# Fewer block products in the output projection of a hybrid encoder layer

## The chip, the cores and the metric

The kernel runs on one core of a Trainium2 chip. Its engines each have an instruction queue of their own, worked off in order: TensorE (PE; its weight loads are listed as PEld), VectorE (DVE), ScalarE (ACT), GpSimd (POOL) and SyncE (SP, which here only starts transfers). The metric is the device time of one execution in microseconds. The kernel before took 1609.84 us, the median of three executions (1609.48 to 1610.66).

## The reference

For 256 tokens of width 4096 the layer computes

```
xn    = RMSNorm(x) * norm_g
h     = xn @ w_in                    # 4096 x 14336: c_val, c_glu, c_gate, q, k, v, a_gate
conv  = silu(LayerNorm(dwconv31(c_val * sigmoid(c_glu)))) * silu(c_gate)
attn  = dilated window attention of 16 heads of 128 (three patterns) * silu(a_gate)
y     = x + concat(conv, attn) @ w_out            # 4096 x 4096
```

all in float32. The change concerns the last line, the product of the 256 x 4096 mixed matrix with `w_out`.

## The kernel before

**Products.** Every product is made of matmuls that hold a 128x128 piece of the activations and stream 128x512 of weights. To keep float32 accuracy each operand is split into a high part, rounded to the fast format fp32r (a cast on ACT), and a low part, the rest (a subtraction on DVE). One block product is three matmuls: high by high, low by high, high by low.

**Groups, steps, pairs.** Weights come in groups of 1024 columns: 14 groups of `w_in` (index 0 to 13), then 4 of `w_out` (14 to 17). A group runs over 32 steps of 128 rows of the weight, each step has 2 token halves (s) x 2 column halves (e) x 3 = 12 matmuls. Weights are loaded by SP as pairs of steps (1 MB, `raw`, 3 buffers) and split three steps ahead (`AHEAD`) into `wh` and `wl` (L197, L198). Four accumulators of 128x512 are in use, another four banks of the accumulator memory ("side") serve the attention.

**The mixed matrix.** Its 32 column blocks (k = 0 to 31, 128 columns each, held as 128 x 256 tokens) are the activations of the output groups. Blocks 0 to 15 are the 16 heads, 16 to 31 the conv path. They are split by `mix_split_gen` (L526, L527) into `mh` and `ml`, in the order 0 to 31, and the output groups use them in that order. A conv block is ready once its gate has come out of the last two input groups (12 and 13, kind "gate"), been turned by 16 small ACT copies per 512 columns (L308) and multiplied in on DVE (L410).

**What sets the order.** The program writes each engine's queue by hand. The loop over steps emits matmuls and splits, and at the end of each step calls `pump`, which lets three lanes of side work (attention and gates, mixed splits, conv) emit instructions up to a quota of estimated time for DVE and ACT. Nothing is reordered at run time: an instruction that waits holds up all behind it on its engine.

Of the kernel before, what the change touches and what calls it, by code (L numbers as in the profile page):

```python
# [11 lines left out]
F32 = mybir.dt.float32  # L12
F32R = mybir.dt.float32r
# [4 lines left out]
P = 128  # L18
S = 256
D = 4096  # L20
KT = D // P
# [23 lines left out]
GROUPS += [("gate", gp, C_GATE + 1024 * gp, C_GATE + 1024 * gp + 512) for gp in range(2)]  # L45
N_IN = len(GROUPS)
GROUPS += [("out", og, 1024 * og, 1024 * og + 512) for og in range(4)]

VECS = {"conv_b": 0, "ln_g": 16, "ln_b": 32, "q_g": 48, "k_g": 49}

# [54 lines left out]
def layer_kernel(  # L105
# [5 lines left out]
    vecs,  # L111
    conv_w,
    bias_rows,
    out,
):
    nc = tc.nc
    xs = x[0].rearrange("(s p) d -> p s d", p=P)
# [5 lines left out]
    def t4(name):  # L123
        return sb.tile([P, 4, 256], F32, tag="c4", bufs=15, name=name)
# [48 lines left out]
    def load_pair(j, cuts=(0, 2048), between=None):  # L173

        g, jj = divmod(j, n_pairs)
        if g >= NG:
            return
        if groups[g][0] == "out":
            jj = (jj + n_pairs // 2) % n_pairs
        rt = sb.tile([P, 2048], F32, tag="raw", bufs=RAW, name=f"raw{j}")  # L180
        raw_tiles[j] = rt.rearrange("p (k c) -> p k c", k=2)
        for lo, hi in zip(cuts, cuts[1:]):
            nc.sync.dma_start(rt[:, lo:hi], w[g, jj, :, lo:hi])
            if between and hi == 1024:
                between()

    w_split = {}

    def split_w(n):
        if n >= NG * KT:  # L190
            return
        j, kk = divmod(n, 2)
        src = raw_tiles[j][:, kk]
        wh = sb.tile([P, 1024], F32R, tag="wh", bufs=AHEAD + 1, name=f"wh{n}")
        wl = sb.tile([P, 1024], F32R, tag="wl", bufs=AHEAD + 1, name=f"wl{n}")
        if n:
            nc.scalar.copy(wh, src)  # L197
            nc.vector.tensor_sub(wl, src, wh.bitcast(F32))  # L198
        else:
            a, b = slice(0, 512), slice(512, 1024)  # L200
            nc.vector.tensor_copy(wh[:, a], src[:, a])
            split_x(0)
            nc.scalar.copy(wh[:, b], src[:, b])
            for c in (a, b):
                nc.vector.tensor_sub(wl[:, c], src[:, c], wh[:, c].bitcast(F32))
        w_split[n] = (wh, wl)
        if kk == 1:
            del raw_tiles[j]
            load_pair(j + RAW)
# [307 lines left out]
    mh, ml = {}, {}  # L517
    progress = {"in": -1}

    def mix_split_gen():  # L520
        for kk in range(KT):
            while not (kk in mix_ready and progress["in"] >= kk + 2):
                yield
            h, l = new_split(kk, "m")
            src = mix_ready[kk]
            nc.scalar.copy(h, src)  # L526
            nc.vector.tensor_sub(l, src, h.bitcast(F32))  # L527
            mh[kk], ml[kk] = h, l
            yield 335

    fg, mix_lane, conv_lane = Lane(3), Lane(1), Lane(1)
    fg.add(setup_gen())
# [18 lines left out]
    def add_out(g, e, s, acc, queues=(nc.sync,)):  # L551

        c, n = groups[g][2 + e], 512 // len(queues)
        for i, queue in enumerate(queues):
            t = xr_tiles[(g, e)][:, s, n * i : n * i + n]
            nc.vector.tensor_add(t, t, acc[:, n * i : n * i + n])  # L556
            queue.dma_start(out[0][P * s : P * s + P, c + n * i : c + n * i + n], t)

    def evacuate(g, e, accs):
        kind, idx = groups[g][:2]  # L560
        rstd = state.get("rstd")
        if kind == "out":
            for s in range(2):
                add_out(g, e, s, accs[s])
            return
        if kind == "conv" and e == 1:
            pair = state["sig"]
        else:
            tile_ = t4(f"{kind}{idx}_{e}")
            pair = tile_.rearrange("p a b -> p (a b)").rearrange("p (s c) -> p s c", s=2)  # L570
        for s in range(2):
            t = pair[:, s, :]
            if kind == "conv" and e == 0:
                nc.scalar.activation(t, accs[s], AF.Sigmoid, scale=rstd[s])
                state["sig"], state["sig_tile"] = pair, tile_
            elif kind == "conv":
                nc.vector.scalar_tensor_tensor(t, accs[s], rstd[s], t, op0=ALU.mult, op1=ALU.mult)
            elif kind == "gate" or (kind == "agv" and e == 0):
                nc.scalar.activation(t, accs[s], AF.Silu, scale=rstd[s])
# [22 lines left out]
    def last_products(n):  # L602

        g, k = divmod(n, KT)
        wh, wl = (t[:, 512:] for t in w_split[n])
        for s in range(2):
            a = accs[(g, 1)][s]
            hs, ls = (t[:, P * s : P * s + P] for t in (mh[k], ml[k]))
            nc.tensor.matmul(a, hs, wh, start=False, stop=False)
            nc.tensor.matmul(a, ls, wh, start=False, stop=False)  # L610
            nc.tensor.matmul(a, hs, wl, start=False, stop=True)
            add_out(g, 1, s, a, (nc.scalar, nc.sync) if s else (nc.sync,))

    def products(n, e, part):

        g, k = divmod(n, KT)
        if k == 0 and part == 0:
            accs[(g, e)] = [
                ps.tile([P, 512], F32, tag="acc", bufs=4, name=f"acc{g}_{e}_{s}") for s in range(2)
            ]  # L620
        if g < n_in:
            h, l = xh[k], xl[k]
        else:
            while k not in mh:
                pump()
            h, l = mh[k], ml[k]
        wp = w_split[n][part][:, 512 * e : 512 * e + 512]
        for s in range(2):
            a = accs[(g, e)][s]
            hs, ls = h[:, P * s : P * s + P], l[:, P * s : P * s + P]  # L630
            if part == 0:
                nc.tensor.matmul(a, hs, wp, start=k == 0, stop=False)  # L632
                nc.tensor.matmul(a, ls, wp, start=False, stop=False)  # L633
            else:
                nc.tensor.matmul(a, hs, wp, start=False, stop=k == KT - 1)  # L635
        if part == 1:
            if k == KT - 1:
                evacuate(g, e, accs.pop((g, e)))
            if e == 1:
                del w_split[n]  # L640

    nc.scalar.dma_start(first_x, x_cols[:, 0 : KT + S])
    xT[0] = first_x[:, KT:]
# [11 lines left out]
    split_w(0)  # L655
    split_x(1)
    split_w(1)
    for n in range(NG * KT):
        g, k = divmod(n, KT)
        if g == n_in - 1:  # L660
            progress["in"] = k
        elif g >= n_in:
            progress["in"] = KT + 2
        if groups[g][0] == "out" and k in (8, 12):
            e = (k - 8) // 4
            c = groups[g][2 + e]
            t = t4(f"xr{g}_{e}").rearrange("p a b -> p (a b)").rearrange("p (s c) -> p s c", s=2)
            nc.sync.dma_start(t, xs[:, :, c : c + 512])
            xr_tiles[(g, e)] = t
        if n == 0:  # L670
            for part in range(2):
                for e in range(2):
                    products(n, e, part)
            for m in (2, 3):
                split_x(m)
                split_w(m)
            rstd_steps = finish_rstd()
        else:
            products(n, 0, 0)
            if k == KT - 1:  # L680
                products(n, 0, 1)
# [5 lines left out]
            split_w(n + AHEAD)  # L687
            if k < KT - 1:
                products(n, 0, 1)
            elif n < NG * KT - 1:  # L690
                products(n, 1, 0)
                products(n, 1, 1)
            else:
                last_products(n)
        if n % 4 == 0 and 12 + n < KT:
            load_xT(12 + n, 4, nc.sync)
        if n in XN_LOAD:
# [7 lines left out]
        elif n == 29:  # L705
            list(rstd_steps)
        pump()

def _layout(i):
# [55 lines left out]
```

## Time and profile before

| | |
|---|---|
| median of three executions | 1609.84 us |
| the profiled execution, its own time | 1610.65 us |
| its span, first to last instruction | 1608.9 us |
| PE busy | 1602.5 us of the span |
| DVE busy | 1072.5 us |
| ACT busy | 926.4 us |
| input groups end, output groups begin on PE | 1256.6 us from the start |
| last matmul starts | 1604.57 us |

Busy times are from the profiled execution. "Idle before" in a row of the groups is the time the engine sat still just before instructions of that group, followed by what released it. A duration is an instruction's own; where an engine overlaps the end of one with the start of the next, the distance between starts is shorter than the duration. Matmuls overlap most: each lasts some 0.39 us, yet they start about 0.23 us apart.

### The profile page before, as it was taken

Reading aid. Unit: us, or ns where it says so; the run is one execution under the profiler, and the core shown is the slowest. Engines: PE = TensorE matmul, PEld = TensorE weight load, DVE = VectorE, ACT = ScalarE, POOL = GpSimd, SP = SyncE. Lnnn points to the kernel's source line nnn. Section 1 sums busy time; section 2 is a strip of 40 time slices with the busy share of each in tenths; the row PEclk is TensorE's granted clock in tenths of the full one; section 3 lists DMA queues with packets and bytes.
Section 4 is the critical chain, followed back from the end, with each engine's and each line's share of the span. In section 5 each row is a group of like instructions: output and inputs, shape, how many; then the busy total and the mean of one; then the engine's idle time right before and its main releaser. Section 6 shows DMA issues by size and latency. Waiting matters only on the chain.

```text
span 1608.9 us, 18840 instructions
## 1 busy us (share of the span) xinstructions
PE 1602.5 (100%) x7058; PEld 1326.6 (82%) x7058; DVE 1072.5 (67%) x1442; ACT 926.4 (58%) x1413; POOL 0.2 (0%) x4
## 2 busy tenths in 40 slices
PE   9999999999999999999999999999999999999999
PEld 7888888888888888888888888888888888888887
DVE  6658888888888888678756555555465665454543
ACT  6763544545453456774778756774767963333332
POOL 0000000000000000000000000000000000000000
PEclk9999999999999999999999999999999999999999
DMA  9755555555555555545555555455555556566662
GB/s 372 291 185 201 191 189 203 185 185 206 187 205 184 196 197 193 193 168 199 185 195 187 187 198 197 174 189 202 184 198 188 196 204 231 207 228 216 216 229 105
DMA packets 52892, 323.53 MB, mean 201 GB/s; under 512 B 5792, under 2 KB 8480, under 8 KB 16192
## 3 DMA queue, kind: packets, MB, share of 16 engines
q1 hardware_dynamic: 52512, 322.05, 56.0%
q8 instruction: 55, 0.90, 0.2%
q10 hardware_dynamic: 288, 0.28, 0.1%
q14 instruction: 37, 0.30, 0.1%
HBM read 318.08 MB, written 4.23 MB: 200 GB/s over the span
## 4 chain that ended last, share of the span: by engine, by line
PE 98%; ACT 1%; DMA 0%; issue 0%; DVE 0%; DVEq 0%
PE acc L632 32%; PE acc L633 32%; PE acc L635 32%; PE psc L469 1%; PE po L508 1%; ACT cT L394 0%; ACT wh L197 0%; DMA first_x<-in_x_cols_dram 0%; ACT qk L308 0%; DVE wl L198 0%; DVE xr L556 0%; DVE qk L449 0%; ACT xh L245 0%; PE vapm L366 0%; PE mupm L366 0%
## 5 line engine op out<-in xcount | busy, mean ns | idle before, releaser
L198 DVE TENSOR_TENSOR wl<-raw,wh 128x1024 fp32r<-128x1024 f32 x575 | 703.6, 1224 | 514.3 <-ACT wh L197 510.4
L197 ACT CAST wh<-raw 128x1024 fp32r<-128x1024 f32 x575 | 604.9, 1053 | 638.4 <-PE acc L633 449.4
L632 PE MATMUL acc<-wh,xh 128*128 128x512 f32 x1792 | 703.9, 393 | 1.0 <-ACT xh L245 1.0
L633 PE MATMUL acc<-wh,xl 128*128 128x512 f32 x1792 | 698.6, 390 | 0.0
L635 PE MATMUL acc<-wl,xh 128*128 128x512 f32 x1792 | 484.1, 389 | 0.0
L632 PEld LDWEIGHTS acc<-wh,xh 128*128 128x128 f32 x1792 | 336.9, 188 | 71.0 <-ACT xh L245 1.3
L633 PEld LDWEIGHTS acc<-wh,xl 128*128 128x128 f32 x1792 | 337.0, 188 | 70.4 <-DVE xl L246 0.2
L635 PEld LDWEIGHTS acc<-wl,xh 128*128 128x128 f32 x1792 | 336.8, 188 | 70.5
L340 DVE SCALAR_TENSOR_TENSOR cT<-conv,wT,cT 128x241 f32<-128x241 f32 (+14 forms) x480 | 201.6, 471 | 0.0
L632 PE MATMUL acc<-wh,mh 128*128 128x512 f32 x510 | 198.4, 389 | 0.0
L633 PE MATMUL acc<-wh,ml 128*128 128x512 f32 x510 | 198.4, 389 | 0.0
L635 PE MATMUL acc<-wl,mh 128*128 128x512 f32 x510 | 137.5, 389 | 0.0
L633 PEld LDWEIGHTS acc<-wh,ml 128*128 128x128 f32 x510 | 95.8, 188 | 19.9
L635 PEld LDWEIGHTS acc<-wl,mh 128*128 128x128 f32 x510 | 95.7, 188 | 19.8
L632 PEld LDWEIGHTS acc<-wh,mh 128*128 128x128 f32 x510 | 95.7, 188 | 19.8
L499 ACT COPY pr<-turn_p 32x128 f32<-32x128 f32 x256 | 75.9, 296 | 5.9 <-DVE turn_p L493 2.4
L308 ACT COPY qk<-turn_q 32x256 f32<-32x256 f32 x64 | 25.9, 404 | 1.2
L308 ACT COPY qk<-turn_k 32x256 f32<-32x256 f32 x64 | 25.8, 403 | 1.2 <-DVE turn_k L300 0.2
L308 ACT COPY gate<-turn_g 32x256 f32<-32x256 f32 x64 | 25.9, 404 | 1.0
L308 ACT COPY agv<-turn_ag 32x256 f32<-32x256 f32 x64 | 25.8, 404 | 1.0
L308 ACT COPY conv<-turn_a 32x256 f32<-32x256 f32 x64 | 25.8, 403 | 1.1
L483 ACT ACTIVATE pr<-pr,nm 128x256 f32<-128x256 f32 x32 | 16.0, 502 | 2.5 <-DVE nm L480 2.4
(128 smaller groups left out, 402.2 us busy)
## 6 DMA issues: line engine op xcount, KB each, us to landing
raw<-in_w_dram SPq DMA_DIRECT2D x286, 1024.0 KB, 4.8
x<-in_x_dram SPq DMA_DIRECT2D x8, 512.0 KB, 7.4
xr<-in_x_dram SPq DMA_DIRECT2D x8, 512.0 KB, 5.8
out_dram<-xr SPq DMA_DIRECT2D x15, 256.0 KB, 5.2
xT<-in_x_cols_dram SPq DMA_DIRECT2D x7, 512.0 KB, 7.3
T<-bias_dram SPq DMA_DIRECT2D x16, 192.0 KB, 5.0
raw<-in_w_dram SPq DMA_DIRECT2D x3, 512.0 KB, 6.5
raw<-in_w_dram SPq DMA_DIRECT2D x2, 256.0 KB, 4.2
```

The lines of the kernel that those rows point to most:

```text
L197: nc.scalar.copy(wh, src)
L198: nc.vector.tensor_sub(wl, src, wh.bitcast(F32))
L308: nc.scalar.copy(dst[32 * b : 32 * b + 32, :, :, to, :], backwards(v) if flip else v)
L340: nc.vector.scalar_tensor_tensor(c[:, t, lo:hi], a[:, t, lo + sh : hi + sh], wT[:, ch, k : k + 1], c[:, t, lo:hi], op0=ALU.mult, op1=ALU.add,)
L469: nc.tensor.matmul(psc[:, it, :], qt[hg][:, hh, P * it : P * it + P], kt[hg][:, hh, :], start=True, stop=True,)
L483: nc.scalar.activation(pi[:, it, :], pi[:, it, :], AF.Exp, bias=nm[:, it : it + 1], accum_out=z[:, it : it + 1],)
L499: nc.scalar.copy(dst[32 * b : 32 * b + 32, :, :, 3 - a, :], backwards(blocks[32 * a : 32 * a + 32, :, :, b, :]),)
L508: nc.tensor.matmul(po[:, :S], vt[hg][:, jt, hs], pT[:, jt, :], start=jt == 0, stop=jt == 1)
L632: nc.tensor.matmul(a, hs, wp, start=k == 0, stop=False)
L633: nc.tensor.matmul(a, ls, wp, start=False, stop=False)
L635: nc.tensor.matmul(a, hs, wp, start=False, stop=k == KT - 1)
```

## The change

In the output groups, 6 of the 16 pairs of steps (`FUSED`: pairs 0 to 5, the columns of heads 0 to 11) are no longer computed as eight block products. A pair is a 2x2 by 2x2 block product: A11, A21 are the token halves of its first mixed block, A12, A22 of its second; B11, B12 are the column halves of its first weight step, B21, B22 of its second. Seven products of sums replace the eight (Winograd's form): S1 = A21+A22, S2 = S1-A11, S3 = A11-A21, S4 = A12-S2 on the mixed side, made once; T1 = B12-B11, T2 = B22-T1, T3 = B22-B12, T4 = B21-T2 on the weight side, made for every group on DVE. The sums are split into high and low parts like the plain operands. M1, M5, M6 and M7 collect in four more accumulators over the six pairs (the "side" and "acc" banks swap roles by group), and `add_more` folds them into the loaded x (`xr`) before the other four accumulators are added.

The ten other pairs stay plain. The pairs go in a new order, `OUT_ORDER`, plain and fused mostly in turn, and the mixed columns are split in that order, so the first to be split are blocks 16 to 19 of the conv path. The weight splits of the output run through `Out.step`, which emits the next split as soon as the tiles in use leave room (8 tiles of 128x1024; 10 from slot 10 of the first output group on).

```diff
+FUSED = (0, 1, 2, 3, 4, 5)
+OUT_ORDER = (8, 9, 0, 10, 1, 11, 2, 6, 3, 7, 4, 12, 5, 13, 14, 15)
+W_SLOTS, W_MORE = 8, 2
...
     def mix_split_gen():
-        for kk in range(KT):
-            while not (kk in mix_ready and progress["in"] >= kk + 2):
+        for i in range(KT):
+            j, odd = OUT_ORDER[i // 2], i % 2
+            kk = 2 * j + odd
+            while not (kk in mix_ready and progress["in"] >= i + 2):
                 yield
+            if j in FUSED:
+                if odd:
+                    yield from mix_fuse(j)
+                continue
...
+    def mix_fuse(j):
+        a0, a1 = mix_ready[2 * j], mix_ready[2 * j + 1]
+        a11, a21, a12, a22 = a0[:, :P], a0[:, P:], a1[:, :P], a1[:, P:]
+        sums = t2(f"mix_sums{j}")
+        s1, s2, s3, s4 = (sums[:, P * i : P * i + P] for i in range(4))
+        nc.vector.tensor_add(s1, a21, a22)
+        nc.vector.tensor_sub(s2, s1, a11)
+        yield 400
+        nc.vector.tensor_sub(s3, a11, a21)
+        nc.vector.tensor_sub(s4, a12, s2)
+        yield 400
...
+        for (h, l), src in zip(parts, (a11, s1, a1, sums[:, P:])):
+            nc.scalar.copy(h, src)
+            nc.vector.tensor_sub(l, src, h.bitcast(F32))
+            yield 300, 300
...
+        def step(self, most=W_SLOTS):
+            if not self.todo or sum(self.held.values()) + self.todo[0][0] > most:
+                return False
+            _, f, u = self.todo.popleft()
+            f()
...
+            def one():
...
+                nc.vector.tensor_sub(t13, r[:, 1:4:2, :], r[:, 0:2, :])
+                h, l = both("b", r[:, 0:3:2, :])
+                low(h, l, r[:, 0:3:2, :])
...
+            def two():
...
+                h, l = both("t13", t13)
+                nc.vector.tensor_sub(t24[:, 0, :], r[:, 3, :], t13[:, 0, :])
+                low(h, l, t13)
...
+            def three():
...
+                nc.vector.tensor_sub(t24[:, 1, :], r[:, 2, :], t24[:, 0, :])
+                hl = halves("b22s", "b22")
+                nc.scalar.copy(hl[:, 0, :], r[:, 3, :])
+                low(hl[:, 0, :], hl[:, 1, :], r[:, 3, :])
...
+            def four():
+                h, l = both("t24", kept["t24"])
+                low(h, l, kept["t24"])
...
+            rows = (
+                (more["m1"], "a11", "b11", ""), (one["c11"], "a12", "b21", "b"),
+                (more["m5"], "s1", "t1", ""), (more["m7"], "s3", "t3", "t13"),
+                (one["c12"], "s4", "b22", "b22"),
+                (more["m6"], "s2", "t2", ""), (one["c21"], "a22", "t4", "t24"),
+            )
+            for i, (acc, an, bn, freed) in enumerate(rows):
+                self.before()
+                own = acc in more.values()
+                self.triple(acc, a[an], self.parts.pop((u, bn)), own and first, own and last)
...
+        def add_more(self, g, more):
+            r = [[xr_tiles[(g, e)][:, s, :] for e in range(2)] for s in range(2)]
+            m1, u, v = t2(f"m1s{g}"), t2(f"us{g}"), t2(f"vs{g}")
+            nc.scalar.copy(m1, more["m1"])
+            nc.vector.tensor_add(r[0][1], r[0][1], more["m5"])
...
+    progress["in"] = KT + 2
+    out.run()
```

ACT at the seam between the last input group and the first output group, in the kernel before: `gate1_1` is the last tile that comes out of the input groups, `mh15` and `mh16` are blocks of the mixed matrix, the COPY rows turn gate tiles, the CAST rows of line 197 split output weights.

```order
L579 ACTIVATE gate1_1_9722<-acc13_1_0_8961,rstd_834 128x512
L579 ACTIVATE gate1_1_9722<-acc13_1_1_8962,rstd_834 128x512
L308 COPY gate0_0_8917<-turn_g0_9552 32x2x4x32 x2
L197 CAST wh451_9735<-raw225_9592 128x1024
L526 CAST mh15_9743<-agv3_0_7579 128x256
L308 COPY gate0_0_8917<-turn_g0_9552 32x2x4x32 x2
...
L197 CAST wh454_9806<-raw227_9686 128x1024
L526 CAST mh16_9812<-cT0_1086 128x256
```

Blocks 0 to 14 have been split ahead of these rows. The same place after the change: `oh`, `bh`, `t13h` and `b22s` are high parts of output weights, `mh0`, `mh1` and `mx0` the parts of the first fused pair's mixed side.

```order
L616 ACTIVATE gate1_1_9670<-acc13_1_1_8962,rstd_834 128x512
L313 COPY gate0_0_8917<-turn_g0_9465 32x2x4x32 x2
L313 COPY gate0_1_8936<-turn_g1_9600 32x2x4x32 x4
L539 CAST mh16_9686<-cT0_1086 128x256
...
L562 CAST mh0_9805<-agv0_0_3472 128x128
L313 COPY gate1_0_9651<-turn_g2_9684 32x2x4x32 x2
L562 CAST mh0_9805<-mix_sums0_9770 128x128
L562 CAST mh1_9807<-agv0_0_3472 128x256
L313 COPY gate1_0_9651<-turn_g2_9684 32x2x4x32 x2
L313 COPY gate1_1_9670<-turn_g3_9799 32x2x4x32 x2
L562 CAST mx0_9809<-mix_sums0_9770 128x384
```

No block of the mixed matrix is split ahead of `gate1_1` any more; the first, block 16, is the first output pair's, and between `gate1_1` and `mx0` stand 30 copies, and 48 up to `mx1`, the same tile of the second fused pair.

DVE in the first output group after the change, from the last weight split of the plain pair in slot 7 to that of the fused pair in slot 8 (`ml6`, `ml7`, `mx3` are the low parts of that pair's mixed side):

```order
L707 TENSOR_TENSOR ol7_1_10092<-raw231_9965,oh7_1_10091 128x1024
L738 TENSOR_TENSOR t13_8_10100<-raw232_9992 128x1024
L726 TENSOR_TENSOR bl_8_10103<-raw232_9992,bh_8_10102 128x1024
...
L726 TENSOR_TENSOR b22s_8_10136<-raw232_9992,b22s_8_10136 128x512
L563 TENSOR_TENSOR ml6_10152<-agv1_0_4805,mh6_10151 128x128
L563 TENSOR_TENSOR ml6_10152<-mix_sums3_10109,mh6_10151 128x128
L563 TENSOR_TENSOR ml7_10154<-agv1_0_4805,mh7_10153 128x256
L563 TENSOR_TENSOR mx3_10155<-mix_sums3_10109,mx3_10155 128x384
L540 TENSOR_TENSOR ml14_10165<-agv3_0_7579,mh14_10164 128x256
L726 TENSOR_TENSOR t24l_8_10169<-t24_8_10115,t24h_8_10168 128x1024
```

The splits of the mixed side now stand among those of the weights; in the kernel before, this place of the queue held four 128x1024 splits for two pairs and nothing else but the last conv blocks.

More of the change, by code (lines that the diff above doesn't have):

```diff
@@ L113, in layer_kernel @@
     bias_rows,
-    out,
+    y,
 ):
@@ L178, in load_pair @@
         if groups[g][0] == "out":
-            jj = (jj + n_pairs // 2) % n_pairs
+            jj = (OUT_ORDER[jj] + n_pairs // 2) % n_pairs
         rt = sb.tile([P, 2048], F32, tag="raw", bufs=RAW, name=f"raw{j}")
@@ L187, in layer_kernel, with ws @@
     w_split = {}
+    def ws(name):
+        return sb.tile([P, 1024], F32R, tag="ws", bufs=W_SLOTS, name=name)
     def split_w(n):
-        if n >= NG * KT:
-            return
         j, kk = divmod(n, 2)
         src = raw_tiles[j][:, kk]
-        wh = sb.tile([P, 1024], F32R, tag="wh", bufs=AHEAD + 1, name=f"wh{n}")
-        wl = sb.tile([P, 1024], F32R, tag="wl", bufs=AHEAD + 1, name=f"wl{n}")
+        wh, wl = ws(f"wh{n}"), ws(f"wl{n}")
         if n:
@@ L518, in layer_kernel @@
     progress = {"in": -1}
+    mx = {}
     def mix_split_gen():
-        for kk in range(KT):
-            while not (kk in mix_ready and progress["in"] >= kk + 2):
+        for i in range(KT):
+            j, odd = OUT_ORDER[i // 2], i % 2
+            kk = 2 * j + odd
+            while not (kk in mix_ready and progress["in"] >= i + 2):
                 yield
+            if j in FUSED:
+                if odd:
+                    yield from mix_fuse(j)
+                continue
             h, l = new_split(kk, "m")
@@ L529, in mix_split_gen @@
             yield 335
+    def mix_fuse(j):
[9 more added lines that the diff above has]
+        yield 400
+        b0, b1 = new_split(2 * j, "m"), new_split(2 * j + 1, "m")
+        more = sb.tile([P, 2, 512], F32R, tag="c4", bufs=15, name=f"mx{j}")
+        parts = [[b[:, :P] for b in b0], [b[:, P:] for b in b0], b1]
+        parts.append([more[:, i, : 3 * P] for i in range(2)])
+        for (h, l), src in zip(parts, (a11, s1, a1, sums[:, P:])):
+            nc.scalar.copy(h, src)
+            nc.vector.tensor_sub(l, src, h.bitcast(F32))
+            yield 300, 300
+        names = {"a11": parts[0], "s1": parts[1]}
+        names["a12"] = [b[:, :P] for b in b1]
+        names["a22"] = [b[:, P:] for b in b1]
+        for i in range(3):
+            names[f"s{i + 2}"] = [more[:, hl, P * i : P * i + P] for hl in range(2)]
+        mx[j] = names
     fg, mix_lane, conv_lane = Lane(3), Lane(1), Lane(1)
@@ L556, in add_out @@
             nc.vector.tensor_add(t, t, acc[:, n * i : n * i + n])
-            queue.dma_start(out[0][P * s : P * s + P, c + n * i : c + n * i + n], t)
+            queue.dma_start(y[0][P * s : P * s + P, c + n * i : c + n * i + n], t)
     def evacuate(g, e, accs):
@@ L561, in evacuate @@
         rstd = state.get("rstd")
[L562 to L565, printed above, removed]
         if kind == "conv" and e == 1:
@@ L600, in layer_kernel @@
     accs = {}
[L602 to L612, printed above, removed]
     def products(n, e, part):
@@ L620, in products @@
             ]
[L621 to L626, printed above, removed]
+        h, l = xh[k], xl[k]
         wp = w_split[n][part][:, 512 * e : 512 * e + 512]
@@ L642, in layer_kernel @@
+    out = Out()
     nc.scalar.dma_start(first_x, x_cols[:, 0 : KT + S])
@@ L657, in layer_kernel @@
     split_w(1)
-    for n in range(NG * KT):
+    for n in range(n_in * KT):
         g, k = divmod(n, KT)
@@ L661, in layer_kernel @@
             progress["in"] = k
[L662 to L669, printed above, removed]
         if n == 0:
@@ L686, in layer_kernel @@
                 split_x(n + 3)
-            split_w(n + AHEAD)
+            if n + AHEAD < n_in * KT:
+                split_w(n + AHEAD)
+            else:
+                out.step()
             if k < KT - 1:
                 products(n, 0, 1)
-            elif n < NG * KT - 1:
+            else:
                 products(n, 1, 0)
                 products(n, 1, 1)
-            else:
-                last_products(n)
         if n % 4 == 0 and 12 + n < KT:
```

143 lines of the change are left out of this document (added).

## The prediction

> **What bounds the kernel now.** I read the page's first part, then a table of stretches, then the waits.
>
> ```profile
> PE 1602.5 (100%) x7058; PEld 1326.6 (82%) x7058; DVE 1072.5 (67%) x1442; ACT 926.4 (58%) x1413; POOL 0.2 (0%) x4
> ...
> 1257.00:1267.00 10.00, 10.00 (x46) 8.29 (x45) 5.63 (x7) 9.73 (x19) 0.00 (x0) 1.00 0.51 199
> 1267.00:1300.00 33.00, 33.00 (x147) 27.31 (x147) 23.68 (x36) 31.23 (x60) 0.00 (x0) 1.00 0.62 224
> 1340.00:1580.00 240.00, 240.00 (x1060) 198.72 (x1060) 115.38 (x101) 92.83 (x88) 0.00 (x0) 1.00 0.62 219
> ...
> DVE wl L198 <- ACT wh L197: 510.4, 501, 3.9
> ACT wh L197 <- PE acc L633: 449.4, 332, 3.4
> ```
>
> PE never rests. The columns after the stretch are PE, PEld, DVE, ACT: from 1340 to 1580 PE is busy 240 of 240 us, DVE 115, ACT 93, and the waits say that DVE waits for ACT's casts and ACT for PE to release buffers. There a matmul removed is time saved. But the first 43 us of the output (1257 to 1300) are another matter: ACT is 97% and 95% busy, with no wait shown on PE. That is the stage to watch.
>
> **What the change removes.** One matmul's price is the distance between starts:
>
> ```profile
> 1228.97 0.39 PE L632 MATMUL acc<-wh,xh 128*128 128x512 f32 x1
> ...
> 1231.69 0.39 PE L632 MATMUL acc<-wh,xh 128*128 128x512 f32 x1
> ```
>
> Twelve matmuls lie between these rows: 2.72 us, or 0.2267 each. A plain pair has 24 (5.44 us), a fused one 21 (4.76 us). Six pairs in four groups drop 72: **-16.3 us**.
>
> **What it adds.** The prices are distances between starts in a stretch without waits:
>
> ```profile
> 1267.48 0.42 DVE L410 TENSOR_TENSOR cT<-cT,gate 128x256 f32<-128x256 f32 x1
> 1267.82 0.70 DVE L300 STREAM_TRANSPOSE turn_g<-gate 128x512 f32<-128x512 f32 x1
> ...
> 1272.28 0.41 DVE L410 TENSOR_TENSOR cT<-cT,gate 128x256 f32<-128x256 f32 x1
> 1272.62 1.21 DVE L198 TENSOR_TENSOR wl<-raw,wh 128x1024 fp32r<-128x1024 f32 x1
> 1273.75 0.41 DVE L527 TENSOR_TENSOR ml<-cT,mh 128x256 fp32r<-128x256 f32 x1
> ...
> 1257.32 1.28 ACT L579 ACTIVATE gate<-acc,rstd 128x512 f32<-128x512 f32 x2
> 1258.62 0.81 ACT L308 COPY gate<-turn_g 32x256 f32<-32x256 f32 x2
> 1259.45 1.05 ACT L197 CAST wh<-raw 128x1024 fp32r<-128x1024 f32 x1
> 1260.41 0.40 ACT L526 CAST mh<-agv 128x256 fp32r<-128x256 f32 x1
> 1260.83 1.65 ACT L308 COPY gate<-turn_g 32x256 f32<-32x256 f32 x4
> 1262.51 1.05 ACT L197 CAST wh<-raw 128x1024 fp32r<-128x1024 f32 x1
> ...
> L203 ACT CAST wh<-raw 128x512 fp32r<-128x512 f32 x1 | 0.6, 627 | 0.3 <-DMA raw<-in_w_dram 0.3
> L205 DVE TENSOR_TENSOR wl<-raw,wh 128x512 fp32r<-128x512 f32 x2 | 1.3, 683 | 0.0
> ```
>
> DVE: 1.13 us for 128x1024 (1272.62 to 1273.75) and 0.335 for 128x256; on the line through both, 0.60 for 512 (I take 0.61), 0.47 for 384, 0.20 for 128. The last size has no row: it costs between half of 0.335 and all of it. ACT: 0.415 a copy, 1.05 for a 1024-wide cast, 0.41 for 256, 0.63 for 512; for 384 I take 0.51 (between the last two) and for 128, 0.30 (0.20 to 0.41).
>
> *Groups 15 to 17.* A fused pair costs DVE four 1024-wide instructions (t13 and three low parts) and three 512-wide ones, a plain pair two of 1024. One of each: 6 x 1.13 + 3 x 0.61 = 8.6 us, against 45 x 0.2267 = 10.2 on PE. ACT has 5 x 1.05 + 0.63 = 5.9. The rest of a group falls where plain pairs stand together (slots 13 to 15, and 0, 1 of the next, 27.2 us of PE): 10 splits 11.3, eight instructions of `add_more` and four of `add_out`, each at most the 0.68 us of this row, 8.2, in all 19.5.
>
> ```profile
> L556 DVE TENSOR_TENSOR xr<-xr,acc 128x512 f32<-128x512 f32 x12 | 7.7, 680 | 0.0
> ```
>
> So three groups are hidden under PE at **0**, with 1.6 us to spare per two slots. The tightest buffer is t24: its cast may start when the plain pair's first step has been read, 2.72 + 5 x 0.68 = 6.1 us ahead of its use, for 1.05 + 1.13 of work. Without cover the excess would come once per fused pair, 18 times.
>
> *Loads.* The bytes stay. 219 GB/s in the steady stretch becomes 219 x 384/366 = 230 where a group takes 366 matmuls instead of 384; the start of the trace moves 415, and DMA is 62% busy. The two `xr` loads now stand together in SP's queue ahead of three weight loads in hand: 0. The end: the last block is still added and stored in two halves, as before, 0 with 0.5 either way.
>
> *Group 14, the first output group.* Here the mixed side is made. Count from T, when PE turns to the output:
>
> ```profile
> 1256.63 0.39 PE L632 MATMUL acc<-wh,mh 128*128 128x512 f32 x1
> ```
>
> In the kernel before, PE goes on at T without a gap, since blocks 0 to 14 were split long ago. In the new order block 16 comes first, and its gate and `gate1_1` must leave ACT first. ACT ends the `gate1_1` pair at 1258.60, T + 2.0; the same casts precede it in both orders. From there ACT's queue holds, up to `mx1` of the second fused pair (slot 4): 48 copies 19.9, eight 1024-wide casts 8.4, two of 512 1.3, eight of 256 3.3, two of 384 1.0, four of 128 1.2: 35.1 us. `mx1` is cast at T + 37.1 at the earliest, since the queue is in order. The fourth product of slot 4 needs its low part (0.47): T + 37.5. Without stalls PE would be there after 102 matmuls, T + 23.1: already **14.4 us late**.
>
> Now DVE. Behind that low part, up to `ml10`, with which slot 12 (the last fused pair) starts, its queue holds 25 instructions of 1024, 12 of 512, 3 of 384, 14 of 256 and 23 of 128: 28.3 + 7.3 + 1.4 + 4.7 + 4.6 = 46.3 us. So slot 12 can't start before T + 83.8. Without stalls it would after 273 matmuls, T + 61.9. In the periods of one plain and one fused pair the reason is plain: 8.6 us of weights, plus mixed side 6 x 0.20 + 0.47 + 3 x 0.335 = 2.7, makes 11.3 against 10.2 on PE. The stall is **21.9 us**, and I add 0.5 for handing over between engines. After slot 12 only plain pairs remain and DVE keeps up, but PE has no slack with which to win anything back.
>
> Bounds of the 21.9: 128-wide at 0.17 each and 1024-wide at 1.10 take off 1.5; 128-wide at 0.335 adds 3.1, 512-wide at the full 0.683 0.9, 1024-wide at its whole duration, 1.21, 2.0. So 20.4 to 27.9.
>
> **Sum**, against the profiled execution (1610.65 us, its span 1608.9): 1610.65 - 16.3 + 21.9 + 0.5 = 1616.8. The median lies 0.8 lower: **1616 us**, slower. Its own range is 1614 to 1622.
>
> **The rivals.** *(a) All hidden.* The seam has cover: ACT and DVE reach T with the mixed blocks ready, as before, and only the removed matmuls count: 1609.84 - 16.3 = 1593.5. For it: PE is busy in every stretch before, with ACT at 97%. Against it: the order has no mixed block split before T. It would decide if the fused parts up to `mx1` were ready by T + 23 instead of T + 37. Chance 0.10.
>
> *(b) Only the seam costs.* DVE falls behind by ACT's 14.4 us but then keeps pace with PE, if its instructions pack some 10% tighter than in the rows above (11.3 to 10.2 a period): 1609.84 - 16.3 + 14.4 = 1607.9, no change. For it: the periods are a near thing. Against: the 128-wide instructions would have to be almost free. Chance 0.15, a third of it below 1606.6.
>
> *(c) PE comes back slow.* At the start of the trace PE does not have its pace at once:
>
> ```profile
> 6.96 0.63 PE L633 MATMUL acc<-wh,xl 128*128 128x512 f32 x1
> 7.38 0.63 PE L632 MATMUL acc<-wh,xh 128*128 128x512 f32 x1
> ...
> 10.39 0.39 PE L632 MATMUL acc<-wh,xh 128*128 128x512 f32 x1
> 10.62 0.39 PE L633 MATMUL acc<-wh,xl 128*128 128x512 f32 x1
> ```
>
> The distance is 0.42 us first, 0.23 from 10.39 on, about 5 us after the first 512-wide matmul. The change makes pauses: at T until `mh16` (2.0 + 6 copies 2.5 + 0.41 = 4.9 us), and some 3 to 4 us at slots 4 and 6. If a pause puts PE back to that pace for 4 us, each costs about 9 x 0.2 = 1.8 us, part of it under ACT's queue: 1 to 5 more, 1617 to 1621; I take 1619. The Trainium skill, "TensorE: Matmul & The Clock Gate", Part 1, says this outright: the clock is halved after an idle window of about 3.4 us and comes back after a busy one. The start of the trace agrees; that a pause in mid-kernel does it, no run here shows, since this PE never paused. By the rule the first pause certainly counts and the sum is 1618 or more; by the rows it may be hidden. Chance 0.15.
>
> *(d) The other groups stall too.* If the tiles in use are too few for a DVE at 84%, each of 18 fused pairs loses perhaps 0.5 us: 1616 + 9 = 1625. Against it the 6.1 us of lead worked out above. Chance 0.08.
>
> **How the numbers follow.** My forecast, DVE and ACT late in group 14 alone, has 0.52. A measurement of this kernel tells 0.2%, or 3.2 us, from no change: faster is under 1606.6, slower over 1613.1. Faster: 0.10 from (a) and 0.05 from (b), 0.15. Same: 0.10 from (b) and 0.05 from the low end of the forecast, 0.15. Slower: the rest, 0.70. The range reaches from 1606 to 1622: it leaves out (a), (d) and little else.
>
> **What would show it.** Right: in the changed profile, PE's stretches are full up to the last input group and from about 85 us into the output to the end, and PE has about 22 us of gaps between, the first some 4 to 5 us, released by ACT (the mixed casts), the later ones by DVE's low parts; the groups list 1464 matmuls in the output. DVE is busy throughout slots 5 to 12 of group 14. Wrong: gaps of less than 16 us in sum, a full PE at slot 12, or gaps in every group. PE starts 0.42 us apart behind a gap would make it (c).

## The result

The changed kernel takes **1620.86 us** (median of four executions, 1619.60 to 1621.34), beside 1609.87 us of the kernel before (now also the median of four, 1609.48 to 1610.66). The ratio is 1.0066, its 95% interval 1.0049 to 1.0084: slower by 11.0 us. The forecast was 1616 us, slower, with a range from 1606 to 1622. The profiled execution took 1620.42 us, with a span of 1618.6 us.

### The profile page after: what moved, and what is told of

It reads as the page before. It is cut to its first block, busy times and chain, and to the rows that moved or that the text cites. A ratio compares the mean times of both kernels' runs of the same rounds, so it can differ in the third digit from the quotient of the medians.

```text
span 1618.6 us, 18988 instructions
## 1 busy us (share of the span) xinstructions
PE 1595.8 (99%) x6986; PEld 1316.1 (81%) x6986; DVE 1195.6 (74%) x1630; ACT 967.0 (60%) x1477; POOL 0.2 (0%) x4
## 4 chain that ended last, share of the span: by engine, by line
PE 94%; DVE 3%; ACT 2%; issue 1%; DMA 0%; DVEq 0%; ACTq 0%
PE acc L652 25%; PE acc L653 25%; PE acc L655 25%; PE c L772 5%; PE c L773 5%; PE c L774 5%; PE m L773 1%; PE m L774 1%; PE m L772 1%; PE psc L474 1%; PE po L513 1%; ACT gate L313 1%; DVE ol L707 0%; DVE t L738 0%; DVE t13l L726 0%
## 5 line engine op out<-in xcount | busy, mean ns | idle before, releaser
L203 DVE TENSOR_TENSOR wl<-raw,wh 128x1024 fp32r<-128x1024 f32 x447 | 547.0, 1224 | 347.9 <-ACT wh L202 347.6
L202 ACT CAST wh<-raw 128x1024 fp32r<-128x1024 f32 x447 | 470.2, 1052 | 463.4 <-PE acc L653 278.0
L772 PE MATMUL c<-oh,mh 128*128 128x512 f32 x320 | 125.9, 393 | 4.9 <-ACT mh L539 4.9
L773 PE MATMUL c<-oh,ml 128*128 128x512 f32 x320 | 125.8, 393 | 0.0
L774 PE MATMUL c<-ol,mh 128*128 128x512 f32 x320 | 125.5, 392 | 0.0
L706 ACT CAST oh<-raw 128x1024 fp32r<-128x1024 f32 x80 | 83.6, 1051 | 55.1 <-PE c L773 39.9
L707 DVE TENSOR_TENSOR ol<-raw,oh 128x1024 fp32r<-128x1024 f32 x80 | 96.5, 1223 | 24.8 <-ACT oh L706 18.9
L772 PEld LDWEIGHTS c<-oh,mh 128*128 128x128 f32 x320 | 60.8, 190 | 17.9 <-ACT mh L539 5.3
L773 PEld LDWEIGHTS c<-oh,ml 128*128 128x128 f32 x320 | 60.9, 190 | 13.1 <-DVE ml L540 0.3
L774 PEld LDWEIGHTS c<-ol,mh 128*128 128x128 f32 x320 | 60.8, 190 | 12.7
```

What stands on the lines that cost most here:

```text
L772: nc.tensor.matmul(acc, a[0], b[0], start=start, stop=False)
L773: nc.tensor.matmul(acc, a[1], b[0], start=False, stop=False)
L774: nc.tensor.matmul(acc, a[0], b[1], start=False, stop=stop)
```

## The profile after

The first part of the page, beside that of before:

```profile
PE 1595.8 (99%) x6986; PEld 1316.1 (81%) x6986; DVE 1195.6 (74%) x1630; ACT 967.0 (60%) x1477; POOL 0.2 (0%) x4
```

PE has 72 matmuls fewer and 6.7 us less of busy time, not 16.3; DVE has 123 us more. The time by stretches (start and end; PE, PEld, DVE, ACT and POOL busy with the count of instructions; granted TensorE clock; share of the DMA engines; GB/s):

```profile
1260.00:1280.00 20.00, 17.73 (x63) 12.57 (x63) 14.86 (x30) 19.04 (x44) 0.00 (x0) 0.91 0.29 106
1280.00:1300.00 20.00, 16.08 (x55) 12.00 (x56) 17.48 (x32) 17.33 (x32) 0.00 (x0) 0.83 0.31 105
1300.00:1320.00 20.00, 16.67 (x72) 13.17 (x72) 19.93 (x36) 12.35 (x22) 0.00 (x0) 1.00 0.47 161
1320.00:1340.00 20.00, 19.06 (x84) 15.41 (x84) 19.93 (x31) 11.47 (x18) 0.00 (x0) 1.00 0.70 260
1340.00:1360.00 20.00, 17.99 (x72) 14.14 (x71) 18.49 (x30) 12.58 (x20) 0.00 (x0) 0.91 0.47 161
1360.00:1400.00 40.00, 40.00 (x178) 33.15 (x177) 32.86 (x37) 19.63 (x21) 0.00 (x0) 1.00 0.64 235
1400.00:1500.00 100.00, 100.00 (x443) 82.84 (x442) 85.54 (x90) 53.00 (x56) 0.00 (x0) 1.00 0.66 233
1500.00:1600.00 100.00, 100.00 (x442) 82.81 (x442) 84.32 (x88) 53.20 (x56) 0.00 (x0) 1.00 0.61 220
```

Everything happens in the first output group. At full pace 20 us hold 88 matmuls; the first five rows hold 63, 55, 72, 84 and 72. ACT is full at first (19.04 of 20), DVE afterwards (19.93 of 20, twice). From 1360 on PE is as full as before. One of these stretches tells more than its busy time: from 1280 to 1300 PE is 80% busy but has only 62% of its matmuls, and the clock column shows 0.83. The rows of PE say why (start, duration; in brackets the idle time before, and its releaser):

```profile
1261.34 0.67 PE L772 MATMUL c<-oh,mh 128*128 128x512 f32 x1 [4.86 <-ACT mh L539]
...
1282.79 0.80 PE L772 MATMUL m<-t24h,mx 128*128 128x512 f32 x1 [2.80 <-ACT t24h L722]
...
1307.36 0.50 PE L773 MATMUL m<-bh,ml 128*128 128x512 f32 x1 [2.40 <-DVE ml L563]
...
1341.77 0.50 PE L772 MATMUL m<-bh,mh 128*128 128x512 f32 x1 [1.25 <-ACT mh L562]
1343.03 0.50 PE L773 MATMUL m<-bh,ml 128*128 128x512 f32 x1 [0.76 <-DVE ml L563]
...
1345.02 0.63 PE L772 MATMUL m<-t13h,mh 128*128 128x512 f32 x1
1345.44 0.63 PE L773 MATMUL m<-t13h,ml 128*128 128x512 f32 x1
...
1614.29 0.39 PE L774 MATMUL c<-ol,mh 128*128 128x512 f32 x1
```

PE waits 4.86 us at the seam for the first mixed cast, then for weight and mixed parts, last at slot 12 (1343.03, the second matmul of the last fused pair in this group). Behind the pauses of 4.86 and 2.80 us, and behind the two at slot 12, matmuls start 0.42 us apart for 3 to 6 us; behind the one of 2.40 us they do not. The last matmul starts 9.72 us later than in the kernel before (1604.57). Since 16.3 us of matmuls are gone, 26.0 us were lost on the way.

What DVE and ACT did at the points that the prediction named:

```profile
1282.77 1.23 DVE L726 TENSOR_TENSOR t24l<-t,t24h 128x1024 fp32r<-128x1024 f32 x1 [2.31 <-ACT t24h L722]
...
1293.48 0.51 ACT L562 CAST mx<-mix_sums 128x384 fp32r<-128x384 f32 x1
...
1295.31 0.55 DVE L563 TENSOR_TENSOR mx<-mix_sums,mx 128x384 fp32r<-128x384 f32 x1
...
1307.02 0.28 DVE L563 TENSOR_TENSOR ml<-agv,mh 128x128 fp32r<-128x128 f32 x1
1307.22 0.28 DVE L563 TENSOR_TENSOR ml<-mix_sums,mh 128x128 fp32r<-128x128 f32 x1
...
1318.44 0.28 DVE L563 TENSOR_TENSOR ml<-agv,mh 128x128 fp32r<-128x128 f32 x1
...
1342.69 0.28 DVE L563 TENSOR_TENSOR ml<-agv,mh 128x128 fp32r<-128x128 f32 x1
```

T, when PE turns to the output, is 1256.33 here. The cast `mx1` starts at T + 37.15, its low part at T + 39.0, `ml10` at T + 86.4. One plain and one fused pair take DVE 11.42 us (1307.02 to 1318.44), against 10.2 on PE. The first row is the last point before `ml10` at which DVE waits more than 0.2 us for another engine: it needs the cast `t24h` of the first fused pair, in slot 2. From there to `ml10` (1282.77 to 1342.69) DVE is busy 59.44 of 59.92 us.

## The experiments

The theory to be tested has three parts: the 26 us are lost in the first output group alone, because the mixed columns used first are split last; ACT's queue and then DVE's set the end of that stage; and a slow pace of PE behind pauses comes on top. The rivals: the fused pairs cost something in every group, ACT alone makes the stall, or the order of the pairs alone does.

### The order alone

```diff
-FUSED = (0, 1, 2, 3, 4, 5)
+FUSED = ()
```

> The new order of pairs and of the mixed splits, but no fused pair: FUSED is empty, so every pair takes 24 matmuls and the computation is the one of before. My theory (the seam has no cover, and ACT is late there): PE again waits 4.9 us at T for the first mixed cast, then for more casts while ACT empties its 48 copies, 19.9 us, with 2.9 us of casts per pair (2 x 1.05 + 2 x 0.41) against 5.44 on PE: by slot 5 ACT is at 19.9 + 6 x 2.9 = 37 us where PE would be at 27, so 5 to 10 us of gaps in sum, and 1.8 for a slow pace behind the first. DVE has 4 x 1.13 + 4 x 0.335 = 5.9 us for two plain pairs against 10.9 on PE and makes no gap. In all 1616 to 1622 us. The rival, that the delay comes from the fused work alone and the order is free: 1609 to 1611, no gap at T.

Measured: 1617.77 us, ratio 1.0046 (1.0033 to 1.0058): 7.6 us slower than before with not one product less or more. Its row of the first output matmul, and two stretches:

```profile
1261.41 0.79 PE L772 MATMUL c<-oh,mh 128*128 128x512 f32 x1 [4.84 <-ACT mh L539]
...
1260.00:1280.00 20.00, 18.59 (x73) 14.96 (x73) 13.18 (x22) 18.86 (x40) 0.00 (x0) 0.86 0.35 120
1280.00:1300.00 20.00, 20.00 (x89) 16.42 (x89) 14.05 (x24) 18.39 (x36) 0.00 (x0) 1.00 0.56 198
```

The time fell in the range, but by fewer gaps than expected: the pause of 4.84 us, some 2 us of slow pace behind it, and nothing later, though ACT is still full (18.39 of 20). Without fused pairs ACT's casts come just in time. So of the 26 us the order alone accounts for 7.6, and the other 18 need the fused pairs in this group.

### First output group plain

The first output group keeps the old order and its plain pairs; the sums of the mixed side are made behind its splits, and the fused pairs begin with the second output group. The mixed side also takes fewer instructions here: each fused pair's four sums are split by one 512-wide cast and one low part, and its other parts come from the plain splits.

```diff
+def out_order(og):
+    return OUT_ORDER if og else tuple(range(16))
+
+def is_fused(og, j):
+    return og > 0 and j in FUSED
...
-        for i in range(KT):
-            j, odd = OUT_ORDER[i // 2], i % 2
-            kk = 2 * j + odd
-            while not (kk in mix_ready and progress["in"] >= i + 2):
+        for kk in range(KT):
+            while not (kk in mix_ready and progress["in"] >= kk + 2):
...
+        for j in FUSED:
+            yield from mix_fuse(j)
```

> The first output group stays as before (its order of pairs 0 to 15, mixed blocks split in that order ahead of T, all pairs plain), the sums of the mixed side are made during it, and only groups 15 to 17 use fused pairs, in the order of the change: 54 matmuls fewer, 12.2 us at 0.2267. My theory (the loss of 26 us is all in the first output group, the other three hide their fused parts at 0): 1609.9 - 12.2 = 1597.6, no gap at T or later; the added 24 additions, 6 casts and 6 low parts lie under a DVE and an ACT that are 48% and 39% busy in that stretch. If fused groups cost something of their own (rival d, 0.5 us for each of 18 pairs): 1606. If fused pairs save nothing at all: 1610.

Measured: 1598.74 us, ratio 0.9925 (0.9913 to 0.9937): 11.5 us faster than before, 22 us faster than the change. Its stretches:

```profile
1260.00:1280.00 20.00, 20.00 (x89) 16.53 (x89) 13.62 (x19) 18.57 (x36) 0.00 (x0) 1.00 0.52 186
...
1360.00:1400.00 40.00, 40.00 (x178) 33.10 (x178) 38.59 (x48) 23.57 (x27) 0.00 (x0) 1.00 0.64 236
1400.00:1500.00 100.00, 100.00 (x443) 82.81 (x442) 84.79 (x92) 52.76 (x56) 0.00 (x0) 1.00 0.63 231
```

PE is full in all of them, also where DVE is 96% busy. The profiled span is 12.0 us shorter than that of before, for 12.2 us of matmuls. So in groups 15 to 17 the fused parts are hidden at nothing, within the spread of the executions (1597.40 to 1598.99), and the rival by which every fused pair costs half a microsecond is out.

### Without the sums of the mixed side

The four sums S1 to S4 are left out, and the parts are cast from the mixed columns themselves.

```diff
-        sums = t2(f"mix_sums{j}")
+        sums = mixA[j // 2].rearrange("p a b -> p (a b)")
+        sums = sums[:, 512 * (j % 2) : 512 * (j % 2) + 512]
...
-        nc.vector.tensor_add(s1, a21, a22)
-        nc.vector.tensor_sub(s2, s1, a11)
...
-        nc.vector.tensor_sub(s3, a11, a21)
-        nc.vector.tensor_sub(s4, a12, s2)
```

> The changed kernel without the four sums of the mixed side: 24 additions of 128x128 on DVE are left out and the parts are cast from the mixed columns themselves, so the output is another one; casts, low parts, matmuls and loads stay. If DVE's queue sets slot 12 (my theory), the 16 additions behind the second fused pair's last low part, 0.20 us each, take off 3.2 us: 1617.7, with gaps only smaller, and the low part of ml10 about 44 us behind that of mx1 instead of 47. If ACT or PE's own slow pace sets it, nothing changes: 1620.9.

Measured: 1614.97 us, ratio 1.0030 (1.0019 to 1.0041), 5.9 us faster than the change instead of 3.2. DVE's period, and PE's slot 12:

```profile
1315.59 0.83 DVE L560 TENSOR_TENSOR ml<-agv,mh 128x128 fp32r<-128x128 f32 x3
...
1326.08 0.83 DVE L560 TENSOR_TENSOR ml<-agv,mh 128x128 fp32r<-128x128 f32 x3
...
1338.72 0.50 PE L770 MATMUL m<-bh,ml 128*128 128x512 f32 x1 [0.76 <-DVE ml L560]
1339.06 0.40 PE L771 MATMUL m<-bl,mh 128*128 128x512 f32 x1
1339.29 0.39 PE L769 MATMUL c<-bh,mh 128*128 128x512 f32 x1
```

The period falls from 11.42 to 10.49 us, 0.93 for four sums, not the 0.80 that I had reckoned. Slot 12's second matmul starts 4.3 us earlier (1338.72 against 1343.03), and no slow pace follows: the next rows are 0.34 and 0.23 apart. PE's pause before the pair is also shorter (0.74 instead of 1.25 us); that this is why is not shown. The missing slow pace is the rest of the gain. Of the 4.3 us, 3.3 are DVE's way from the low part of `mx1` to that of `ml10` (44.1 us, as expected, instead of 47.4), and 1.0 us was won ahead of `mx1`, which the expectation had left out. With DVE's queue shortened the stage ends sooner by as much as the queue got shorter: DVE sets it.

### Without the gate copies

ACT's copies of turned gates are left out for three of four channel blocks, so the gates stay unturned.

```diff
-                nc.scalar.copy(
-                    dst[32 * b : 32 * b + 32, :, :, to, :], backwards(v) if flip else v
-                )
+                if name not in ("turn_g1", "turn_g2", "turn_g3"):
+                    nc.scalar.copy(
+                        dst[32 * b : 32 * b + 32, :, :, to, :], backwards(v) if flip else v
+                    )
```

> The changed kernel with ACT's copies of the turned gates left out for channel blocks 1 to 3 (the copies that still stand behind T, 48 of them, and the last ones ahead of it), so the output is another one; the order of all other instructions stays. It tells apart how much of the stall is ACT's and how much DVE's. My theory: both share it. DVE is busy 29.65 + 47.10 of the 86.4 us from T to slot 12, so it idles 9.65 us, all of it behind ACT; without 48 x 0.415 = 19.9 us of copies that idle time goes, and what DVE's own 76.8 us of work leave remains: 1620.9 - 9.7 = 1611.2, with a first gap of 2.4 us instead of 4.9. If ACT alone made the stall: 1620.9 - 19.9 = 1601. If ACT had no part: 1620.9.

Measured: 1610.63 us, ratio 1.0002 (0.9993 to 1.0010), 10.2 us faster than the change. Its eleven executions spread from 1608.41 to 1613.41 us, and the profiled one took 1611.97 us, 8.5 us less than the profiled one of the change. 46 of the 48 copies left out stand behind T. The stretches from T to the low part that slot 12's second matmul waits for (`ml10`, to its start in the first table and to its end in the second), first of the changed kernel:

```profile
1256.30:1295.30 39.00, 29.29 (x99) 20.74 (x99) 29.65 (x55) 36.90 (x78) 0.00 (x0) 0.87 0.31 110
1295.30:1342.70 47.40, 41.45 (x177) 32.69 (x176) 47.10 (x79) 29.15 (x48) 0.00 (x0) 1.00 0.56 199
```

then without the copies:

```profile
1255.90:1295.00 39.10, 32.89 (x126) 25.64 (x126) 36.85 (x67) 21.45 (x36) 0.00 (x0) 0.91 0.38 138
1295.00:1334.80 39.80, 35.15 (x150) 27.55 (x148) 39.50 (x69) 25.46 (x45) 0.00 (x0) 1.00 0.57 208
```

In the changed kernel DVE is busy 76.75 of 86.4 us up to slot 12, without the copies 76.35 of 78.9. DVE's idle time falls from 9.65 to 2.55 us, by 7.1 us, and that is most of the 8.5 us between the profiled executions; it does not go to nothing, and the first gap is 2.85 us instead of the expected 2.4. So ACT's 19 us of copies behind T were worth some 8 to 10 us of time, about the idle time of DVE that they caused; behind that stands DVE's own work of 76.4 us, against 61.9 us in which PE would do its part. ACT alone isn't the cause.

### Keeping PE at work in the pauses

Matmuls of a zero block are added where PE pauses.

```diff
+        def keep_warm(self, acc, n, start):
+            for _ in range(n):
+                nc.tensor.matmul(acc[:, :S], zero, xh[KT - 1], start=start, stop=start)
...
+                if (u, i) == (2, 5):
+                    self.keep_warm(acc, 24, True)
+                elif (u, i) == (12, 0):
+                    self.keep_warm(acc, 12, False)
...
+                    if (u, k, e) == (0, 0, 0):
+                        self.keep_warm(one["c11"], 40, True)
```

> The changed kernel with matmuls of a zero block put where PE pauses: 40 of 256 columns ahead of the first output product, 24 ahead of the sixth product of slot 2, 12 ahead of the first of slot 12; they add work and change nothing in the output. If the pauses bring back the pace of 0.42 us (rival c on top of the forecast), the rows behind slot 12's gap are 0.23 apart instead of 0.42 and the end comes 1.7 us earlier, since no later stall hides it: 1619.1; the slow rows in slots 0 and 2 lie ahead of DVE's work, which sets slot 12, and give at most 2 us more, 1617. If the pace is not set by the pauses, the rows stay 0.42 apart and the time stays at 1620.9 or rises by what the added matmuls take, up to 1622.

Measured: 1618.36 us (1617.35 to 1618.82), ratio 1.0049 (1.0036 to 1.0061). The ratio's interval overlaps with the changed kernel's, the times themselves do not: 2.5 us between the medians, 1.6 between the profiled executions. PE at slot 12:

```profile
1340.48 1.58 PE L775 MATMUL m<-xh,zero 128*128 128x256 f32 x12
1341.93 0.50 PE L778 MATMUL m<-bh,mh 128*128 128x512 f32 x1
1343.19 0.50 PE L779 MATMUL m<-bh,ml 128*128 128x512 f32 x1 [0.76 <-DVE ml L565]
1343.53 0.39 PE L780 MATMUL m<-bl,mh 128*128 128x512 f32 x1
1343.75 0.39 PE L778 MATMUL c<-bh,mh 128*128 128x512 f32 x1
```

The low part that slot 12 waits for comes no sooner (1343.19 against 1343.03), but behind it the matmuls run at 0.23 us apart instead of 0.42 at once: added work made the kernel faster. The pace is whole as well at the seam and behind the filled pause in slot 2, yet slot 12 starts no earlier. PE reaches slot 2 sooner and waits 1.24 us there for ACT's cast `mh`, where the changed kernel has no wait; behind this pause and two of 0.41 and 0.19 us a new slow stretch appears (1276.61 to 1279.76). So of the three slow stretches taken away only the last, 1.7 us, lies on the path; the others fall in time that PE would otherwise spend waiting for ACT and DVE.

### More fused pairs

With the first group plain, seven pairs (`FUSED` 0 to 6) and eight pairs (0 to 7) are fused in the other three groups.

```diff
-FUSED = (0, 1, 2, 3, 4, 5)
-OUT_ORDER = (8, 9, 0, 10, 1, 11, 2, 6, 3, 7, 4, 12, 5, 13, 14, 15)
+FUSED = (0, 1, 2, 3, 4, 5, 6)
+OUT_ORDER = (8, 0, 9, 1, 10, 2, 11, 3, 12, 4, 13, 5, 14, 6, 7, 15)
```

> As the kernel with a plain first output group, with seven fused pairs instead of six in groups 15 to 17 (8, 0, 9, 1, 10, 2, 11, 3, 12, 4, 13, 5, 14, 6, 7, 15): 63 matmuls fewer than before, 9 fewer than with six. DVE per group 7 x 6.35 + 9 x 2.26 + 8.2 = 73.0 us against 82.3 on PE. If DVE's total of a group decides, all is hidden: 1598.7 - 9 x 0.2267 = 1596.7. If the six pairs were already at the limit of what the order hides (pairs alternate, and the spare time lies at a group's end only), each of the three groups loses about what the added pair takes on DVE over a plain one, 4.1 us less the 1.6 of slack: 1600 to 1604.

Measured: **1596.69 us**, ratio 0.9917 (0.9904 to 0.9931), 13.7 us faster than before and the best of this study; 2.05 us below six pairs, where nine matmuls are 2.04. The executions of each kernel spread over 1.1 to 1.6 us, so the agreement is closer than these medians can vouch for. In its stretch PE stays full with DVE at 90%:

```profile
1400.00:1500.00 100.00, 100.00 (x442) 82.80 (x442) 89.87 (x95) 55.10 (x59) 0.00 (x0) 1.00 0.64 232
```

For eight pairs the same `OUT_ORDER` serves, in which slots 13 and 14 are then both fused:

> The same with eight fused pairs, two of them side by side in slots 13 and 14: 72 matmuls fewer than before, 18 fewer than with six. DVE per group 8 x 6.35 + 8 x 2.26 + 8.2 = 77.1 us against 81.6 on PE, 94%. If a group's total decides: 1598.7 - 18 x 0.2267 = 1594.6. If the lead of a fused pair's parts decides, the pair of fused slots waits, 2 x 6.35 = 12.7 us of DVE against 2 x 4.76 = 9.5 on PE, some 3 us for each of the three groups: 1601 to 1605, with gaps of PE at slot 14 released by DVE's low parts.

Measured: 1598.96 us, ratio 0.9932 (0.9918 to 0.9946), 2.3 us slower than seven. PE's waits there:

```profile
1434.98 0.50 PE L774 MATMUL m<-t13l,mx 128*128 128x512 f32 x1 [1.36 <-DVE t13l L726]
1437.98 0.50 PE L774 MATMUL m<-t24l,mx 128*128 128x512 f32 x1 [0.53 <-DVE t24l L726]
...
1520.97 0.50 PE L774 MATMUL m<-t24l,mx 128*128 128x512 f32 x1 [0.52 <-DVE t24l L726]
```

and DVE ahead of the first of them, in order: the last adds of the group that ends (L597), between the first and the later fused parts of the next group's slot 1:

```profile
1429.58 1.22 DVE L726 TENSOR_TENSOR bl<-raw,bh 128x1024 fp32r<-128x1024 f32 x1
1430.71 2.47 DVE L597 TENSOR_TENSOR xr<-xr,c 128x512 f32<-128x512 f32 x4
1433.11 0.68 DVE L749 TENSOR_TENSOR t<-raw,t 128x512 f32<-128x512 f32 x1
1433.71 1.22 DVE L726 TENSOR_TENSOR t13l<-t,t13h 128x1024 fp32r<-128x1024 f32 x1
```

The time lies between the two that were expected, 4.4 us over 1594.6 and 2 us under 1601. The forecast of a loss came true, but not at the place named for it: slot 14 itself has no wait. The wait shows in the next group's first fused pair, where DVE has the group's adds between that pair's parts. A group's total, 94% of PE's time by the expectation, doesn't decide. My reading is that the stretch of two fused pairs and the adds behind them does; no run separates the two, and the three waits above, 2.4 us in sum, are not the whole loss. An order that hides eight pairs was not tried: with a plain first and last slot, as the program has them, two fused pairs must be neighbours.

## Why the prediction was right, and where its sizes were off

**The removed matmuls, -16.3 us: right.** Seven pairs against six gave 2.05 us for nine matmuls, the price of 0.2267 us each as far as the spread of the executions allows to tell.

**Groups 15 to 17 at nothing: right.** PE is at 100.00 of 100.00 in both long stretches after, and the kernel with a plain first group gains what its removed matmuls are worth. The tail, at nothing, moved by none either: in both kernels the span ends 4.3 us behind the last matmul's start.

**The stall of the first output group, 21.9 + 0.5 us: the mechanism was right, the size 2.2 us too small, and DVE took over from ACT earlier than I had it.** ACT's end of `gate1_1` plus 35.1 us of its queue put the end of the `mx1` cast at T + 37.1; it started at T + 37.15 and ended at T + 37.7, after ACT had itself waited on the way, 0.34 us for PE (1265.82) and 0.72 us for DVE (1288.42). The low part was to be done at T + 37.5 and was done at T + 39.5, 2.0 us late. It was not waiting for that cast, which had ended 1.3 us before the low part started, but for its turn: I had let DVE follow ACT at once, but DVE had waited for ACT's casts further up (14.86 busy of 20 us from 1260 to 1280), last for `t24h` of the first fused pair, and from there on (1282.77, T + 26.4) its own full queue sets the pace, 11 us earlier than in the prediction. So the 14.4 us by way of `mx1` is not the path that was taken; that it came out near is partly luck, since the cast and DVE's own queue reached the same low part within 1.3 us of each other.

DVE's queue from the low part of `mx1` to the end of that of `ml10`, forecast at 46.3 us, took 47.1; half of the 0.8 us more is the second of the dependent sums, which comes 0.32 instead of 0.20 us behind the first, four times. The handing over to PE took 0.06 us, where I had 0.5. So slot 12's second matmul came at T + 86.7 where T + 84.3 was forecast for its first. It is only the second that needs the low part, and without stalls it would start at T + 62.1, one matmul behind the T + 61.9 of the prediction. The stall is thus 24.6 us, 2.2 more than forecast and within the bounds of 20.4 and 27.9.

**Rival (c), PE comes back slow: it happened, on top of the forecast and not in its place.** I had treated it as another case with 1619; it is a term of the sum, worth 1.7 us at slot 12, near the 1.8 us of its price. With both, 16.3 gained, 22.4 + 2.2 + 1.7 lost and a T that came 0.3 earlier make the 9.7 by which the last matmul starts later. What I missed in weighing it is where a slow pace counts: not at the seam, where I looked, since ACT and DVE are late there anyway, but behind the last pause, where nothing covers it any more.

**The median.** 1616 was 4.9 us too low: 3.6 of it in the profiled execution (1616.8 against 1620.42), from the two terms above less the 0.3 of T, and 1.2 because I took the median 0.8 us below the profiled execution; here it lies 0.4 above.

**Rival (a), all hidden,** is out by the 4.86 us at the seam. **Rival (b), only the seam costs:** DVE's period was 11.42 us, 0.1 over the forecast, so it didn't keep pace. Its price of 14.4 us was reckoned with the fused parts in ACT's queue; the order without them costs 7.6. **Rival (d)** is out by the kernel with a plain first group.

**The signs I named.** The first gap, 4 to 5 us released by ACT, came as said; the later ones are released by DVE's low parts, save one of 2.80 us by ACT's cast `t24h` and two by its casts `mh` (0.42 us in slot 2, 1.25 us at slot 12). About 22 us of gaps was wrong as a sign: PE is idle 16.0 us from T to slot 12's second matmul (the 15.66 us of the two stretches up to 1342.70 and 0.33 more), just at the 16 below which I had called the forecast wrong, though 26 us were lost. Most of the rest lies in matmuls at half pace, which count as busy. The place and the releasers would have been a better sign than the sum of idle time.

## What to carry to other kernels

When a change reorders who needs what first, recount at the seam: write down for each engine's queue what stands ahead of the first piece now needed, and follow it to the last place where the late engine still sets PE's pace. A saving that is hidden in the steady stage can be lost many times over in the one stage where its preparation is made; leaving that stage as it was kept most of the saving here (11.5 of 16.3 us), and one more fused pair in each later group brought 2 us more. Count the added work over the worst stretch of a few steps, not over a whole group.

## What the runs showed of the hardware

**Pauses of less than 3 us can be followed by a slow PE.** Pauses of 2.85 and 2.71 us, as these rows of the kernel without copies show, were followed by matmuls 0.42 us apart:

```profile
1258.90 0.50 PE L773 MATMUL c<-oh,mh 128*128 128x512 f32 x1 [2.85 <-ACT mh L540]
...
1260.71 0.63 PE L775 MATMUL c<-ol,mh 128*128 128x512 f32 x1
1261.14 0.63 PE L773 MATMUL c<-oh,mh 128*128 128x512 f32 x1
...
1286.07 0.50 PE L774 MATMUL m<-bh,ml 128*128 128x512 f32 x1 [2.71 <-DVE ml L564]
1286.41 0.40 PE L775 MATMUL m<-bl,mh 128*128 128x512 f32 x1
...
1288.04 0.63 PE L774 MATMUL m<-t13h,ml 128*128 128x512 f32 x1
1288.47 0.63 PE L775 MATMUL m<-t13l,mh 128*128 128x512 f32 x1
```

So were 1.25 and 0.76 us with one matmul between them (the changed kernel's slot 12), and 1.24, 0.41 and 0.19 us with three matmuls and one between them (slot 2 with the added matmuls), but not 2.40 us alone, nor 0.74 and 0.76 (without the sums). The slow pace may set in a microsecond or two after PE is back: here the first rows are still at or near full pace. The Trainium skill, "TensorE: Matmul & The Clock Gate", Part 1, gives an idle window of about 3.4 us for it; the pause of 4.86 us agrees, but those of 2.71 and 2.85 us show the slow pace below that figure, also when the 0.39 us that the matmul ahead of the pause lasts is added (3.24 us), and here the measurement decides. What exactly is counted, the runs don't settle.

**Small DVE instructions overlap.** A 128x128 subtraction lasts 0.28 us and the next starts 0.20 after it (1307.02 to 1307.22 in the changed kernel), as the estimate between the bounds had it; where one reads what the one ahead wrote, as S2 does with S1, it is 0.32 (1314.57 to 1314.89).
